# RWKV-7 recurrence on one core: grouping the chunk's state products, alternating the masked products, decay totals by head pairs

## The chip, the cores and the metric

The kernel runs on one core of one Trainium2 chip. The metric is device microseconds of one execution; the median of several executions counts. Engines are named as the profile names them: PE is TensorE (PEld its weight loads), DVE is VectorE, ACT is ScalarE, POOL is GpSimd, SP is SyncE. Each engine works through its own list of instructions in order and waits on semaphores for the others.

## What is computed

One two-layer trunk over 256 frames and 2048 features. Layer 0 mixes tokens with RWKV-7, layer 1 with forgetting attention, and each is followed by a SwiGLU. The change touches the recurrence of layer 0 alone: 32 heads of 64 features, each with a 64x64 state that is carried over the frames.

```python
def wkv7_scan(r, w, k, v, a, b):
    # S_t = S_{t-1} diag(w_t) + (S_{t-1} a_t) b_t^T + v_t k_t^T,   y_t = S_t r_t
    def step(S, inp):
        r_t, w_t, k_t, v_t, a_t, b_t = inp
        sa = jnp.einsum('bhij,bhj->bhi', S, a_t)
        S = (S * w_t[:, :, None, :] + sa[..., None] * b_t[:, :, None, :]
             + v_t[..., None] * k_t[:, :, None, :])
        return S, jnp.einsum('bhij,bhj->bhi', S, r_t)
...
    kk = kk / jnp.maximum(jnp.sqrt(jnp.sum(kk * kk, axis=-1, keepdims=True)), 1e-12)
    k = k * (1.0 + (a - 1.0) * k_a)
    y = wkv7_scan(rh, wh, kh, vh, -kk, kk * ah)
```

## The kernel before, in words

**The stream of large products.** All large weight matrices pass through one planned stream. A weight block of 128x512 is fetched by SP, split by ACT into a rounded high part (`wh`, line 148) and by DVE into the remainder (`wl`, line 149), and then used by six matmuls: for each of two halves of the frames high x high (line 174), high x low (175) and low x high (176). Seven split blocks may stand ready ahead of PE.

**Work between them.** Everything else runs as Python generators. `S.gemm` calls `tick()` after every three large matmuls, and a tick takes each live generator one `yield` further. So the order on every engine is fixed when the program is built: a background matmul sits in PE's list behind the large matmuls that were issued before its tick. Where a loop waits for a generator to get somewhere (`S.until`), it ticks without large matmuls, and background work stands back to back in PE's list. Background work shares four PSUM banks (tiles named `bg`), taken with `S.take` and handed back with `S.give`.

**The recurrence.** The 32 heads are four groups of eight, the 256 frames two halves of two chunks of 64. Eight *units* (group g, half t) pass in order through four generators, each unit with two chunks c: `prepare` builds the decayed keys and the masked products, `solve` and `merge` invert the triangular system of each chunk and head with small 32x32 products, `chain` carries the state over the chunks, and `post` normalises. All this lies beside the stream's products r, w2, a2, g2 and o. With `half = [0:64, 64:128]` of the partitions, chunk c keeps its values on `vs = half[c]` and its keys and its system on `us = half[1 - c]`.

- Line 521 sums the log decays within a chunk (`ps`). Line 523 sums them over a whole chunk for each head (`pc`): eight products with 64 columns of weights each, both chunks as two moving columns. Line 539 turns the totals into `wc` with two ACT instructions per unit.
- Lines 584 to 603 transpose the keys and place them head by head with ACT copies; the last of these, line 603, writes `fkb` in four copies (chunk 0 then chunk 1, even then odd heads).
- Line 611 forms, for chunk c and head h, the product of `fkb` and `far`, both 64 rows high on `us`, into 128 output partitions. Four heads fill one PSUM bank. Line 613 multiplies a bank with the causal mask on DVE and writes `M`. The order is chunk by chunk: bank, one `yield`, mask, next bank.
- Line 765 multiplies `M` with the values and the state in `sv` (128 rows, 64 columns) into the `us` half of a bank `pb`; line 767, for all chunks but the first of a group (12 of 16), multiplies `far` with the state alone (64 rows, 64 columns) into the `vs` half. The two alternate head by head. ACT copies the `us` half (770), line 773 applies the inverse, ACT copies again (775), and lines 778 and 780 form the new state and the output. Line 780 adds to what line 767 wrote.

An f32 product stands in the trace as two matmul records, so the eight products of line 765 for a chunk are 16 records.

Of the kernel before, what the change touches and what calls it, by code (L numbers as in the profile page):

```python
# [11 lines left out]
AF = mybir.ActivationFunctionType  # L12
# [5 lines left out]
P = 128  # L18
# [5 lines left out]
C = 64  # L24
# [9 lines left out]
C_ID, C_TRI, C_IND, C_M, C_E, C_B8, C_LANE, C_I8, C_CAUSAL, C_END = 0, 128, 256, 258, 386, 450, 482, 486, 550, 678  # L34
# [164 lines left out]
def hybrid_kernel(ctx, tc, const, x, a_norm_g, a_mix, a_w_rkv, a_w0, a_w1, a_w2, a_a0, a_a1, a_a2,  # L199
                  a_g1, a_g2, a_k_k, a_k_a, a_r_k, a_lnx_g, a_lnx_b, a_w_o, b_norm_g, b_w_in, b_b_f,  # L200
                  b_qn_g, b_kn_g, b_on_g, b_w_o, f_norm_g, f_w_gu, f_w_d, final_g, out):
    nc = tc.nc
# [33 lines left out]
    S = Stream(tc, ctx, plan, 4)  # L236
    mm = nc.tensor.matmul
# [15 lines left out]
    cst = small.tile([P, C_END], F32, name="cst")  # L253
# [72 lines left out]
    with ExitStack() as actx:  # L326
# [5 lines left out]
        with ExitStack() as bctx:  # L332
# [123 lines left out]
            b = begin()  # L456
# [25 lines left out]
        with ExitStack() as bctx:  # L482
# [22 lines left out]
            half = [slice(0, C), slice(C, P)]  # L505
            hsl = [slice(h * N, h * N + N) for h in range(8)]
# [5 lines left out]
            def prepare():  # L512
                for i, (g, t) in enumerate(order):
# [5 lines left out]
                    ps = yield from S.take()  # L519
                    pc = yield from S.take()  # L520
                    mm(ps[:, :], cst[:, C_TRI : C_TRI + P], tw[:, :], start=True, stop=True)
                    for h in range(8):
                        mm(pc[0:C, 2 * h : 2 * h + 2], tw[:, hsl[h]], cst[:, C_IND : C_IND + 2], start=True, stop=True)
                    kk = u1.tile([P, 512], F32, name="kk")
                    nc.vector.tensor_tensor(kk[:, :], k, vk[:, :], op=ALU.mult)
                    sq = u1.tile([P, 512], F32, name="rr")
# [9 lines left out]
                    nc.scalar.activation(W, ps[:, :], AF.Exp)  # L536
                    nc.scalar.activation(Wi[:, :], ps[:, :], AF.Exp, scale=-1.0)
                    for c in range(2):
                        nc.scalar.activation(wc[half[c], :], pc[0:C, c : 16 + c : 2], AF.Exp)
                    S.give(2)  # L540
                    n8 = u1.tile([P, 8], F32, name="n8")
                    nc.vector.tensor_reduce(n8[:, :], h4(sq[:, :]), AX.X, ALU.add)
# [60 lines left out]
                            nc.scalar.copy(dst, tkv[half[q], :, :])  # L603
                        S.give()
                    yield
                    for c in range(2):
                        us = half[1 - c]
                        for b in range(2):
                            pm = yield from S.take()
                            for h in range(4):  # L610
                                mm(pm[:, h * P : (h + 1) * P], fkb[us, b * 4 + h, :], far[us, b * 4 + h, :], start=True, stop=True)  # L611
                            yield
                            nc.vector.tensor_tensor(
                                M[:, c * 8 + b * 4 : c * 8 + b * 4 + 4, :], pm[:, :].rearrange("p (h n) -> p h n", n=P),
                                cst[:, C_M : C_M + P].unsqueeze(1).broadcast_to([P, 4, P]), op=ALU.mult,
                            )
                            S.give()
# [119 lines left out]
            def chain():  # L737
                nxt = values(0, 0, 0)
                for i, (g, t) in enumerate(order):
# [11 lines left out]
                    for c in range(2):  # L751
                        first = t == 0 and c == 0
                        last = t == 1 and c == 1
                        vs, us = half[c], half[1 - c]
                        sv, vu = nxt
                        vus.append(vu)
                        if c == 0:
                            nxt = values(g, t, 1)
                        elif i < 7:
                            if i:  # L760
                                yield from wait(("gated", i - 1))
                            nxt = values(*order[i + 1], 0)
                        pb = yield from S.take()
                        for h, hs in enumerate(hsl):
                            mm(pb[us, hs], M[:, c * 8 + h, C : 2 * C], sv[:, hs], start=True, stop=True)  # L765
                            if not first:
                                mm(pb[vs, hs], far[us, h, 0:C], sv[us, hs], start=h == 0, stop=False)  # L767
                        yield
                        yield
                        nc.scalar.copy(vu[us, :], pb[us, :])  # L770
                        pu = yield from S.take()
                        for h, hs in enumerate(hsl):
                            mm(pu[us, hs], TT[us, h, :], vu[us, hs], start=True, stop=True)  # L773
                        yield
                        nc.scalar.copy(vu[us, :], pu[us, :])
                        for h, hs in enumerate(hsl):
                            if not last:
                                mm(pu[vs, hs], kb[:, c, hs], vu[:, hs], start=True, stop=True)  # L778
                        for h, hs in enumerate(hsl):
                            mm(pb[vs, hs], M[:, c * 8 + h, 0:C], vu[:, hs], start=first, stop=first or h == 7)  # L780
                        if not last:
                            new = nxt[0][vs, :]
                            w = wc[vs, :].unsqueeze(2).broadcast_to([C, 8, N])
                            if first:
                                nc.vector.tensor_tensor(h4(new), h4(pu[vs, :]), w, op=ALU.mult)
                            else:
                                nc.vector.tensor_tensor(new, pu[vs, :], sv[us, :], op=ALU.add)
                                nc.vector.tensor_tensor(h4(new), h4(new), w, op=ALU.mult)
                        nc.scalar.copy(Y[vs, :], pb[vs, :])
                        S.give(2)  # L790
                        yield
                        yield
# [529 lines left out]
```

## Time and profile before

| | |
|---|---|
| median of 3 executions | 2687.72 us (2664.91 to 2695.59) |
| the profiled execution | 2667.2 us |
| its span, first to last instruction | 2665.4 us |
| mean granted PE clock over the span | 0.989 |
| PEld busy | 80% |
| DVE busy | 63% |
| ACT busy | 55% |
| POOL busy | 3% |
| DMA, mean | 176 GB/s |

The profiled execution is near the fastest of the three, and 20.5 us below their median. A busy PE is not PE at its peak: matmuls are pipelined and their ends are modelled, so the length of a run of matmuls is best read from the start of its first row to the start of the row that follows it. The recurrence fills about 256 to 640 us of the span; what comes before and after it holds no line of the change.

### The profile page before, as it was taken

How to read it: one execution, taken by the hardware profiler on the slowest of the kernel's cores; microseconds unless marked ns; L12 is line 12 of the kernel's file. 1: busy time of each engine (PE TensorE's matmuls, PEld its weight loads, DVE VectorE, ACT ScalarE, POOL GpSimd, SP SyncE). 2: the span in 40 equal slices, each digit the busy share in tenths (PEclk: the TensorE clock that was granted, in tenths of full speed). 3: DMA queues.
4: the chain of work that ended last, by engine and by line, in shares of the span. 5: the costliest groups of instructions: out<-in, count | busy, mean ns of one | idle time of the engine just before them, and what ended most of it. 6: DMA issues, size and time to landing. Idle time of an engine off the chain costs nothing.

```text
span 2665.4 us, 41151 instructions
## 1 busy us (share of the span) xinstructions
PE 2624.3 (98%) x15256; PEld 2142.5 (80%) x15256; DVE 1677.5 (63%) x2977; ACT 1478.7 (55%) x2849; POOL 87.9 (3%) x68
## 2 busy tenths in 40 slices
PE   7999999999999999999999999999999999999998
PEld 6788777777888888888888888888888888888886
DVE  7885876766655555555556677776755555555554
ACT  6665676756655545444445565665655555454443
POOL 0000010000000000000000110110000000000000
PEclk9999998889999999999999999999999999999999
DMA  5676332323666666665557666665566666665554
GB/s 187 193 215 206 99 100 79 92 91 111 178 194 185 193 187 191 187 193 191 192 191 205 202 193 184 196 185 170 174 192 186 192 187 191 187 191 193 196 195 157
DMA packets 253946, 468.48 MB, mean 176 GB/s; under 512 B 22248, under 2 KB 32696, under 8 KB 253744
## 3 DMA queue, kind: packets, MB, share of 16 engines
q1 hardware_dynamic: 251056, 464.58, 57.5%
q8 instruction: 120, 1.97, 0.3%
q10 hardware_dynamic: 2528, 1.26, 0.2%
q14 instruction: 82, 0.67, 0.1%
q0 software_dynamic: 160, 0.00, 0.0%
HBM read 457.37 MB, written 4.23 MB: 173 GB/s over the span
## 4 chain that ended last, share of the span: by engine, by line
PE 95%; ACT 2%; DVE 1%; DMA 1%; issue 1%; SPq 0%; ACTq 0%; POOLq 0%; DVEq 0%
PE mm L174 28%; PE mm L176 28%; PE mm L175 28%; PE bg L611 1%; PE bg L765 1%; PE bg L767 1%; DMA st<-in_a_w_rkv_dram 1%; PE bg L941 1%; ACT xb L592 1%; PE bg L773 1%; PE bg L302 1%; PE bg L778 1%; PE bg L780 0%; ACT Bs L811 0%; PE bg L1174 0%
## 5 line engine op out<-in xcount | busy, mean ns | idle before, releaser
L149 DVE TENSOR_TENSOR wl<-st,wh 128x512 fp32r<-128x512 f32 (+1 forms) x1648 | 1130.2, 691 | 823.1 <-ACT wh L148 817.8
L148 ACT CAST wh<-st 128x512 fp32r<-128x512 f32 (+1 forms) x1648 | 1018.8, 623 | 944.9 <-DVE wl L149 695.7
L174 PE MATMUL mm<-wh,xb 128*128 128x512 f32 x2048 | 803.6, 392 | 0.0
L176 PE MATMUL mm<-wh,xb 128*128 128x512 f32 x2048 | 799.8, 391 | 0.0
L175 PE MATMUL mm<-wl,xb 128*128 128x512 f32 x2048 | 799.4, 390 | 0.0
L174 PEld LDWEIGHTS mm<-wh,xb 128*128 128x128 f32 x2048 | 384.6, 188 | 79.9 <-issue 3.3
L176 PEld LDWEIGHTS mm<-wh,xb 128*128 128x128 f32 x2048 | 384.4, 188 | 79.5
L175 PEld LDWEIGHTS mm<-wl,xb 128*128 128x128 f32 x2048 | 384.7, 188 | 76.0
L174 PE MATMUL mm<-wh,xa 128*128 128x512 f32 x768 | 311.2, 406 | 0.0
L175 PE MATMUL mm<-wl,xa 128*128 128x512 f32 x768 | 307.4, 400 | 0.7 <-DVE wl L149 0.7
L176 PE MATMUL mm<-wh,xa 128*128 128x512 f32 x768 | 306.0, 399 | 0.0
L174 PE MATMUL mm<-wh,hb 128*128 128x512 f32 x448 | 174.3, 389 | 0.0
L175 PE MATMUL mm<-wl,hb 128*128 128x512 f32 x448 | 174.3, 389 | 0.0
L176 PE MATMUL mm<-wh,hb 128*128 128x512 f32 x448 | 174.3, 389 | 0.0
L174 PEld LDWEIGHTS mm<-wh,xa 128*128 128x128 f32 x768 | 146.4, 191 | 30.4 <-issue 1.0
L176 PEld LDWEIGHTS mm<-wh,xa 128*128 128x128 f32 x768 | 146.2, 191 | 30.4 <-DVE xa L854 0.2
L175 PEld LDWEIGHTS mm<-wl,xa 128*128 128x128 f32 x768 | 146.6, 191 | 29.2 <-DVE wl L149 1.5
L175 PEld LDWEIGHTS mm<-wl,hb 128*128 128x128 f32 x448 | 84.1, 188 | 17.5
L174 PEld LDWEIGHTS mm<-wh,hb 128*128 128x128 f32 x448 | 84.1, 188 | 17.4
L176 PEld LDWEIGHTS mm<-wh,hb 128*128 128x128 f32 x448 | 84.1, 188 | 17.4
L1122 POOL TENSOR_TENSOR n<-n,pw 128x8 f32<-128x8 f32 x24 | 45.1, 1882 | 411.4 <-DVE n L1121 411.4
L315 DVE TENSOR_TENSOR x<-mm,x 128x512 f32<-128x512 f32 x58 | 38.0, 685 | 11.6 <-PE mm L176 11.5
(277 smaller groups left out, 2007.7 us busy)
## 6 DMA issues: line engine op xcount, KB each, us to landing
st<-in_f_w_gu_dram SPq DMA_DIRECT2D x352, 512.0 KB
st<-in_f_w_d_dram SPq DMA_DIRECT2D x176, 512.0 KB
st<-in_b_w_in_dram SPq DMA_DIRECT2D x128, 512.0 KB
st<-in_a_w_rkv_dram SPq DMA_DIRECT2D x96, 512.0 KB
st<-in_a_w_o_dram SPq DMA_DIRECT2D x32, 512.0 KB
st<-in_b_w_o_dram SPq DMA_DIRECT2D x32, 512.0 KB
x<-in_x_dram SPq DMA_DIRECT2D x16, 256.0 KB
cb<-cdram SPq DMA_DIRECT2D x4, 1024.0 KB
```

What stands on the lines that cost most here:

```text
L148: nc.scalar.copy(hi[:rows, :n], st)
L149: nc.vector.tensor_tensor(lo[:rows, :n], st, hi[:rows, :n].bitcast(F32), op=ALU.subtract)
L174: nc.tensor.matmul(ps[t][:, :n], xh[:rows, c], wh, start=kt == 0, stop=False)
L175: nc.tensor.matmul(ps[t][:, :n], xh[:rows, c], wl, start=False, stop=False)
L176: nc.tensor.matmul(ps[t][:, :n], xl[:rows, c], wh, start=False, stop=kt == kts - 1)
L302: nc.tensor.transpose(tp[:, i * T + t * P : i * T + (t + 1) * P], src[:, t, c : c + P], ident)
L315: nc.vector.tensor_tensor(X[g][:, t, :], ps[t][:, :], X[g][:, t, :], op=ALU.add)
L592: nc.scalar.copy(dst, tpv[half[q], :, c, :])
L611: mm(pm[:, h * P : (h + 1) * P], fkb[us, b * 4 + h, :], far[us, b * 4 + h, :], start=True, stop=True)
L765: mm(pb[us, hs], M[:, c * 8 + h, C : 2 * C], sv[:, hs], start=True, stop=True)
L767: mm(pb[vs, hs], far[us, h, 0:C], sv[us, hs], start=h == 0, stop=False)
L1122: nc.gpsimd.tensor_tensor(n8[:, :], n8[:, :], pw[:, :], op=ALU.pow)
```

## The change

Three edits in two generators.

In `prepare`, the decay totals are formed for pairs of heads: four products with 128 columns of weights in place of eight with 64. The totals of odd heads then lie on the upper partitions, and `wc` is written with four ACT instructions in place of two.

Also in `prepare`, the masked products take two PSUM banks at once, one for each chunk, and alternate between the chunks head by head. Two masks follow together. The loop goes over two pairs of banks in place of four banks, with a `yield` each, so a unit has two yields there in place of four.

In `chain`, the eight products of line 765 are issued first and the eight of line 767 after them, in place of alternating.

```diff
-                    for h in range(8):
-                        mm(pc[0:C, 2 * h : 2 * h + 2], tw[:, hsl[h]], cst[:, C_IND : C_IND + 2], start=True, stop=True)
+                    for p in range(4):
+                        mm(pc[:, 2 * p : 2 * p + 2], tw[:, p * P : (p + 1) * P], cst[:, C_IND : C_IND + 2], start=True, stop=True)
...
                     for c in range(2):
-                        nc.scalar.activation(wc[half[c], :], pc[0:C, c : 16 + c : 2], AF.Exp)
+                        for q in range(2):
+                            nc.scalar.activation(wc[half[c], q:8:2], pc[half[q], c:8:2], AF.Exp)
...
-                    for c in range(2):
-                        us = half[1 - c]
-                        for b in range(2):
-                            pm = yield from S.take()
-                            for h in range(4):
-                                mm(pm[:, h * P : (h + 1) * P], fkb[us, b * 4 + h, :], far[us, b * 4 + h, :], start=True, stop=True)
-                            yield
+
+                    for b in range(2):
+                        pm = []
+                        for c in range(2):
+                            pm.append((yield from S.take()))
+                        for h in range(4):
+                            for c in range(2):
+                                us = half[1 - c]
+                                mm(pm[c][:, h * P : (h + 1) * P], fkb[us, b * 4 + h, :], far[us, b * 4 + h, :], start=True, stop=True)
+                        yield
+                        for c in range(2):
                             nc.vector.tensor_tensor(
-                                M[:, c * 8 + b * 4 : c * 8 + b * 4 + 4, :], pm[:, :].rearrange("p (h n) -> p h n", n=P),
+                                M[:, c * 8 + b * 4 : c * 8 + b * 4 + 4, :], pm[c][:, :].rearrange("p (h n) -> p h n", n=P),
                                 cst[:, C_M : C_M + P].unsqueeze(1).broadcast_to([P, 4, P]), op=ALU.mult,
                             )
                             S.give()
...
                         for h, hs in enumerate(hsl):
                             mm(pb[us, hs], M[:, c * 8 + h, C : 2 * C], sv[:, hs], start=True, stop=True)
-                            if not first:
+                        if not first:
+                            for h, hs in enumerate(hsl):
                                 mm(pb[vs, hs], far[us, h, 0:C], sv[us, hs], start=h == 0, stop=False)
```

## The prediction, on record before the changed kernel ran

> **What bounds the kernel now.** I read the page's totals and its chain of waits first, then the busy table over the stretch of the recurrence, then PE's timeline inside it.
>
> ```profile
> span 2665.4 us, 41151 instructions
> ...
> PE 95%; ACT 2%; DVE 1%; DMA 1%; issue 1%; SPq 0%; ACTq 0%; POOLq 0%; DVEq 0%
> ```
>
> PE holds 95% of the chain that ended last. Now the busy table for 256 to 660 us: length, busy time of PE, PEld, DVE, ACT and POOL (instructions in brackets), PE's granted clock, DMA share, GB/s.
>
> ```profile
> 256.00:660.00 404.00, 394.84 (x4943) 304.01 (x4942) 292.52 (x622) 274.73 (x678) 32.98 (x25) 0.94 0.31 95
> ```
>
> PE is busy for 394.84 of 404 us, DVE for 292.52 (72%) and ACT for 274.73 (68%). DMA stands at 0.31 of its time, so the weights are no limit here. What shortens PE's list in this stretch shortens the kernel, as long as DVE and ACT keep up. The second thing to see is the clock, 0.94 in place of 1.
>
> PE's timeline shows what line 765 and 767 cost (start, length, engine, line, count of records):
>
> ```profile
> 316.95 1.15 PE L765 MATMUL bg<-sv,xb 128*64 128x64 f32 x16
> 318.03 0.50 PE L175 MATMUL mm<-wl,xa 128*128 128x512 f32 x1
> ...
> 325.16 0.33 PE L765 MATMUL bg<-sv,xb 128*64 128x64 f32 x2
> 325.42 0.32 PE L767 MATMUL bg<-sv,xb 64*64 64x64 f32 x2
> 325.68 0.33 PE L765 MATMUL bg<-sv,xb 128*64 128x64 f32 x2
> ...
> 329.27 0.50 PE L175 MATMUL mm<-wl,xa 128*128 128x512 f32 x1
> ...
> 330.41 1.14 PE L773 MATMUL bg<-vu,TT 64*64 64x64 f32 x16
> 331.48 0.50 PE L176 MATMUL mm<-wh,xa 128*128 128x512 f32 x1
> ```
>
> Alone, the 16 records of line 765 take 318.03 - 316.95 = 1.08 us. Alternating with line 767, each product of two records takes 0.26 us, and the 32 records take 329.27 - 325.16 = 4.11 us. The 16 records of line 773, which have line 767's shape and stay in one shape, take 331.48 - 330.41 = 1.07 us. So the change of shape at every product costs about half of the 4.11 us.
>
> **The change part by part.**
>
> *State products in one run (765, 767).* Per chunk: 1.08 + 1.07 = 2.15 us by the two rows above, in place of 4.11. That is 1.96 us for each of 12 chunks, 23.5 us. Upper end the same: the shapes stay what they are. Lower end 0, if the slowness belonged to line 767 itself; line 773's row speaks against that. ACT, which takes the result, waits for PE here and not PE for ACT: in its group of the stretch (busy time and mean ns, then idle time before it and what ended it) the copy of line 770 waits 36.4 us in all for line 767.
>
> ```profile
> L770 ACT COPY vu<-bg 64x512 f32<-64x512 f32 x16 | 9.3, 582 | 36.6 <-PE bg L767 36.4
> ```
>
> *Granted clock.* The busy table for six of the twelve alternating runs (start and end by the timeline), with the sum of all:
>
> ```profile
> 325.16:329.27 4.11, 4.11 (x33) 3.03 (x33) 2.23 (x7) 0.03 (x1) 0.00 (x0) 1.00 0.01 5
> ...
> 409.59:414.24 4.65, 4.65 (x33) 3.37 (x33) 3.74 (x10) 0.28 (x1) 0.00 (x0) 0.84 0.49 156
> 443.33:447.73 4.40, 4.40 (x34) 3.22 (x33) 3.54 (x8) 4.10 (x11) 1.94 (x1) 0.90 0.19 63
> 497.35:501.46 4.11, 4.11 (x34) 3.03 (x33) 3.59 (x14) 1.31 (x4) 0.00 (x0) 1.00 0.51 150
> ...
> 536.85:543.31 6.46, 6.46 (x34) 4.58 (x33) 1.93 (x4) 0.56 (x3) 0.00 (x0) 0.50 0.00 0
> ...
> 592.60:596.71 4.11, 4.11 (x34) 3.03 (x33) 2.49 (x12) 0.62 (x2) 0.00 (x0) 1.00 0.31 79
> ...
> sum 52.47, PE 52.47 PEld 38.45 DVE 34.64 ACT 17.12 POOL 3.89; mean PE 4.37 PEld 3.20 DVE 2.89 ACT 1.43 POOL 0.32
> ```
>
> The same table for the five stretches of the recurrence in which the granted clock was 0.50:
>
> ```profile
> 412.75:422.99 10.24, 10.24 (x59) 7.96 (x60) 2.60 (x6) 1.78 (x3) 0.24 (x1) 0.50 0.10 34
> 446.88:450.30 3.42, 3.42 (x12) 2.67 (x11) 2.84 (x7) 1.85 (x4) 0.00 (x0) 0.50 0.21 50
> 501.50:508.32 6.82, 6.82 (x34) 5.02 (x34) 0.00 (x0) 2.82 (x5) 0.00 (x0) 0.50 0.28 101
> 525.39:545.87 20.48, 20.48 (x115) 15.17 (x113) 11.44 (x22) 11.42 (x29) 1.95 (x1) 0.50 0.12 35
> 597.07:603.90 6.83, 6.83 (x39) 5.12 (x38) 1.67 (x4) 2.52 (x5) 0.00 (x0) 0.50 0.27 100
> ```
>
> Four of the five drops begin within an alternating run or at most 0.4 us after its end (412.75, 446.88, 501.50, 597.07). The four last 27.3 us, and at half clock half of it is lost: 13.7 us. The fifth (20.48 us) begins in other work at 525.39, but the run at 536.85 lies within it; I count 4 us of its 10.2 as won. All lengths are multiples of 3.41 us, so a drop seems to be decided window by window, and an alternating run of 4.11 us can fill a window where one of 2.15 us can't. I take 17.7 us; ends 0 (the drops come from something that stays) and 23.9 (half of all 47.8 us). The drops need not repeat alike in another execution: the one profiled took 2667.2 us, 20.5 us less than the median of 2687.72.
>
> [...]
>
> *Masked products (611).* One unit, PE with the ACT copies that it waits for:
>
> ```profile
> 308.76 2.38 ACT L603 COPY WW<-bg 64x512 f32<-64x512 f32 x4
> 309.39 0.48 PE L611 MATMUL bg<-xb,WW 64*128 64x128 f32 x2 [0.16 <-ACT WW L603]
> 309.80 0.50 PE L174 MATMUL mm<-wh,xa 128*128 128x512 f32 x1
> 310.23 0.93 PE L611 MATMUL bg<-xb,WW 64*128 64x128 f32 x6
> 311.10 0.69 PE L704 MATMUL bg<-Ti,xb 32*32 32x32 f32 x32
> 311.72 2.60 PE L611 MATMUL bg<-xb,WW 64*128 64x128 f32 x24
> 314.25 1.12 PE L521 MATMUL bg<-tw,cst 128*128 128x512 f32 x2
> 315.31 1.09 PE L523 MATMUL bg<-cst,tw 128*64 128x2 f32 x16
> 316.33 0.69 PE L720 MATMUL bg<-Tt,Xs 32*32 32x32 f32 x32
> ```
>
> And line 611's own records in two equal stretches of its long run:
>
> ```profile
> 312.16:312.72 0.56, 0.56 (x11) 0.56 (x10) 1.00 0.00 0
> 313.10:313.66 0.56, 0.56 (x7) 0.56 (x7) 1.00 0.00 0
> ```
>
> Line 611 takes 0.41 + 0.87 + 2.53 = 3.81 us per unit. The two stretches hold 11 records where the run passes from chunk 0 to chunk 1, hence from one half of the rows to the other, against 7 inside a chunk (records that reach into a stretch are counted). So products on different row halves run side by side, and a change of half costs nothing. Alternating them at every head would double the rate: 16 records as 8 steps of about 0.11 us (2.53/24) and 0.2 us to start (0.87 - 6 x 0.11), 1.1 us for a bank pair, 2.2 per unit, 12.9 us over 8 units. That is the upper end. The lower end takes the alternation as dear as that of 765 and 767, 0.26 us for each of 16 products: 4.2 us per unit, 3 us lost in all.
>
> I take less than the upper end, since the first bank pair now needs all four copies of line 603, where the first bank needed two. They end at 308.76 + 2.38 = 311.14. PE waits there in order, with line 704 and the large products behind it, and ACT's line 708 waits for 704; five of the eight products can follow only then (0.6 us), so line 704 starts at about 311.8, the second pair at 312.4, and the end is 313.5 in place of 314.25. That is 0.7 us per unit, 5.6 us in all.
>
> *Masks (613) and banks.* The same 32 DVE instructions, in pairs:
>
> ```profile
> L613 DVE TENSOR_TENSOR xb<-bg,cst 128x512 f32<-128x512 f32 x32 | 21.6, 687 | 9.3 <-PE bg L611 9.3
> ```
>
> A pair takes 1.4 us, so the second bank of a pair comes free 0.7 us later than it would alone, and two banks are held where one was. `merge` holds a third. PE's next use of a bank may wait a part of that: up to 8 x 0.7 = 5.6 us, none if line 704 or a large product lies between. I take 2 us.
>
> *Decay totals (523, 539).* Line 523 takes 316.33 - 315.31 = 1.02 us for 16 records. It becomes 8 records with twice the weight columns, at the shape of the neighbours, so the change of shape goes too. Ends: half, 0.51 us less per unit (4 us in all), and nothing, if a record costs by its weight columns. I take 1 us. For line 539 the row gives the shortest, median and longest of its 16 instructions in ns:
>
> ```profile
> L539 ACT ACTIVATE wc<-bg x16: 163/170/172, 258.5 to 537.3; 64x8 f32<-64x8 f32 x16
> ```
>
> Sixteen more at 0.17 us are 2.7 us of ACT, with the weight casts of line 148 queued behind them; I count 1 us as exposed, ends 0 and 2.7.
>
> *Less cover.* The stretch loses about 48 us of PE, while DVE and ACT keep their work: 292.52 of 356 us is 82%. Seven split blocks stand ready ahead of PE, so most of it stays hidden. In the alternating runs DVE works 34.64 of 52.47 us; they shrink to 12 x 2.15 = 25.8 us and would hold 17.0 of it in the same proportion. The other 17.6 us must find room elsewhere: ends 0 and 17.6; I take 2 us, since DVE has 111 us free in the stretch.
>
> Sum against the profiled execution: 2667.2 - 23.5 - 17.7 - 5.6 - 1 + 2 + 1 + 2 = 2624.4, rounded to 2624 us. That is 1.6% below it and 2.4% below the median shown.
>
> **The rivals.**
>
> *Masked products at full worth.* If the ACT copies are not what PE waits for, 12.9 in place of 5.6: 2617 us. For it: PE's wait on line 603 in this unit is 0.16 us. Against: its first bank needs two copies only.
>
> *The drops of the clock stay.* Small products remain, and the fifth drop began without an alternating run ahead. Then the 17.7 us are missing: 2642 us. Against: four of five begin with one. [...]
>
> *DVE or ACT becomes the bound.* If the 17.6 us of "less cover" are lost in place of 2: 2640 us. For it: DVE's 72% rises to 82%, and ACT's share likewise. Against: ACT waits for PE in its row, 36.4 us before line 770 alone, and gets those waits back.
>
> *The order changes nothing.* If the 0.26 us per product came from line 767's operands and not from the alternation, 23.5 and 17.7 us are missing: 2666 us. Against: line 773's row.
>
> [...]
>
> **How the numbers follow.** Chances: the forecast 0.56, masked products at full worth 0.09, drops stay 0.15, DVE or ACT 0.12, nothing changes 0.05, slower 0.03. The predicted time is the forecast's, 2624 us. The range, 2604 to 2652, takes in the first four. It reaches up to 10 us over the higher of the two at 2640 and 2642 and down to where all drops go (6 us more) and the masked products bring their full worth (7 us more), with 7 us for what two executions differ by. About 1% is what a measurement of this kernel can tell from no change. The forecast and the first rival are faster by more (0.65), and so are the two at 2640 and 2642 us against the median shown (1.7%), but not against an execution like the profiled one (0.9%); I give two thirds of their 0.27 to faster. So faster 0.83, within 1% 0.14 (with "nothing changes"), slower 0.03.
>
> **What would show it.** Right: line 765 and line 767 as two runs of 16 records, together 2.1 to 2.2 us; no half clock behind them, and a granted clock over 0.97 for the recurrence; line 611 as runs of 16 in 1.1 us, with the first of a unit held up by line 603; line 523 as 8 records in 0.9 us. Wrong: 767 still at 0.26 us a product; half clock behind single runs; PE waiting often for `wl` or `wh`, which would mean that DVE and ACT set the pace; a unit's line 611 over 3.8 us.

## The result, and the profile after

The changed kernel takes 2629.93 us in the median (four executions, 2625.47 to 2637.86) against 2678.70 us for the kernel before (four executions, 2664.91 to 2695.59): a ratio of 0.983, with an interval of 0.980 to 0.987. The profiled execution took 2628.21 us, 39 us less than the profiled one of before. One execution of e2 below, of 5686 us where the nine others took 2674 to 2691, is left out of every figure here. Six lines that matter have new numbers: 603 is now 604, 611 is 615, 613 is 618, 765 is 770, 767 is 773 and 773 is 779.

The page of the changed kernel, its first line and the shares of its chain of waits:

```profile
span 2626.4 us, 41027 instructions
...
PE 92%; ACT 4%; DVE 2%; issue 1%; DMA 1%; POOL 0%; SPq 0%; ACTq 0%; POOLq 0%; DVEq 0%
```

The busy table (length; busy time of PE, PEld, DVE, ACT, POOL; granted clock; DMA share; GB/s) for the recurrence and for what follows it:

```profile
256.00:623.00 367.00, 351.86 (x4897) 278.09 (x4896) 294.88 (x630) 278.13 (x699) 35.90 (x25) 0.99 0.35 107
623.00:2626.00 2003.00, 1990.22 (x9165) 1640.25 (x9163) 1187.20 (x1945) 1042.57 (x1848) 51.28 (x33) 1.00 0.62 189
```

The ends at 660 us (before) and 623 us (changed) do not fall on the same work: the large product of the stream that starts at 660 us before starts at 619.3 us here. By the same products the recurrence is 40.7 us shorter, and what follows it 1 to 2 us longer. DVE and ACT do in 367 us about what they did in 404, so DVE is busy for 80% of the stretch and ACT for 76%. PE still carries the chain, but ACT's share of it rose from 2% to 4% and DVE's from 1% to 2%. PE is idle for 367.00 - 351.86 = 15.1 us there, where it was 9.2 us.

PE's timeline for the state products:

```profile
324.05 1.15 PE L770 MATMUL bg<-sv,xb 128*64 128x64 f32 x16
325.13 1.14 PE L773 MATMUL bg<-sv,xb 64*64 64x64 f32 x16
326.20 0.50 PE L175 MATMUL mm<-wl,xa 128*128 128x512 f32 x1
```

326.20 - 324.05 = 2.15 us. The timeline of one unit's masked products and decay totals, with the ACT copies ahead of them:

```profile
340.01 2.39 ACT L604 COPY WW<-bg 64x512 f32<-64x512 f32 x4
340.64 0.49 PE L615 MATMUL bg<-xb,WW 64*128 64x128 f32 x2
341.06 0.50 PE L174 MATMUL mm<-wh,xa 128*128 128x512 f32 x1
341.49 1.90 PE L615 MATMUL bg<-xb,WW 64*128 64x128 f32 x14
343.32 0.69 PE L709 MATMUL bg<-Ti,xb 32*32 32x32 f32 x32
343.94 1.16 PE L615 MATMUL bg<-xb,WW 64*128 64x128 f32 x16
345.03 1.12 PE L521 MATMUL bg<-tw,cst 128*128 128x512 f32 x2
...
346.45 0.95 PE L523 MATMUL bg<-cst,tw 128*128 128x2 f32 x8
347.26 0.49 PE L174 MATMUL mm<-wh,xa 128*128 128x512 f32 x1
```

The first pair of banks takes 0.42 + 1.83 = 2.25 us and ends 0.9 us after the fourth copy (342.40), the second pair 1.09 us. Line 523 takes 0.81 us.

The busy table for all the stretches of the recurrence with the clock at half:

```profile
310.15:313.56 3.41, 3.41 (x30) 2.60 (x24) 2.03 (x4) 2.60 (x7) 0.00 (x0) 0.50 0.00 0
388.65:392.07 3.42, 3.42 (x9) 2.63 (x9) 3.28 (x8) 3.33 (x8) 0.00 (x0) 0.50 0.02 5
572.97:576.39 3.42, 3.24 (x15) 2.14 (x16) 1.45 (x3) 2.76 (x7) 1.46 (x1) 0.50 0.54 155
sum 10.25, PE 10.07 PEld 7.38 DVE 6.75 ACT 8.69 POOL 1.46; mean PE 3.36 PEld 2.46 DVE 2.25 ACT 2.90 POOL 0.49
```

47.8 us of half clock became 10.25 us. The starts of the stretches lie a whole number of windows apart (388.65 - 310.15 = 78.5 = 23 x 3.413; 572.97 - 388.65 = 184.3 = 54 x 3.413), and so do those of before (446.88 - 412.75 = 34.13 = 10 x 3.413). In each of these two executions all drops of the recurrence start on one grid of 3.413 us. The grid does not start with the kernel: counted in whole windows from the first instruction, the drops lie 2.95 us past one here (310.15), 3.15 us in the kernel before (412.75), and below 2.63 us in e2 (361.03) and 0.23 us in e12 (310.84).

The second of these drops stands behind a wait that the kernel before did not have. Timeline, with the wait in brackets:

```profile
386.19 1.28 DVE L618 TENSOR_TENSOR xb<-bg,cst 128x512 f32<-128x512 f32 x2
...
386.93 1.05 PE L523 MATMUL bg<-cst,tw 128*128 128x2 f32 x8 [1.37 <-DVE xb L618]
```

Line 523 needs the bank that the first of two masks hands back. The first drop follows a window with 2.35 us of masked products, the third a pause of PE of 1.39 us before line 709, for which the profile names no releaser. In the view of waits for this stretch the row of line 523 is new (engine and line, what it waited for, us in total, times, longest):

```profile
PE bg L615 <- ACT WW L604: 2.2, 6, 0.8
...
PE bg L523 <- DVE xb L618: 1.4, 1, 1.4
```

Between the two profiled executions, from start to start in PE's timeline, the state products went from 56.7 to 30.0 us, the masked products from 33.9 to 28.2, line 523 from 9.0 to 7.3.

### The profile page after: what moved, and what is told of

It is laid out like the page before. It is cut to its first block, busy times and chain, and to the rows that moved or that the text cites. A ratio compares the mean times of both kernels' runs of the same rounds, so it can differ in the third digit from the quotient of the medians.

```text
span 2626.4 us, 41027 instructions
## 1 busy us (share of the span) xinstructions
PE 2578.1 (98%) x15192; PEld 2113.7 (80%) x15192; DVE 1674.5 (64%) x2977; ACT 1475.4 (56%) x2865; POOL 91.4 (3%) x68
## 4 chain that ended last, share of the span: by engine, by line
PE 92%; ACT 4%; DVE 2%; issue 1%; DMA 1%; POOL 0%; SPq 0%; ACTq 0%; POOLq 0%; DVEq 0%
PE mm L174 28%; PE mm L176 28%; PE mm L175 28%; PE bg L947 1%; PE bg L779 1%; ACT xb L593 1%; PE bg L770 1%; PE bg L615 1%; PE bg L786 1%; PE bg L302 1%; ACT wh L148 1%; DVE wl L149 1%; PE bg L784 0%; PE bg L773 0%; ACT Bs L817 0%
## 5 line engine op out<-in xcount | busy, mean ns | idle before, releaser
L174 PE MATMUL mm<-wh,xb 128*128 128x512 f32 x2048 | 803.6, 392 | 0.0
L175 PE MATMUL mm<-wl,xb 128*128 128x512 f32 x2048 | 799.5, 390 | 0.0
L174 PEld LDWEIGHTS mm<-wh,xb 128*128 128x128 f32 x2048 | 384.7, 188 | 79.8 <-issue 3.3
L175 PEld LDWEIGHTS mm<-wl,xb 128*128 128x128 f32 x2048 | 384.8, 188 | 75.9
L174 PE MATMUL mm<-wh,xa 128*128 128x512 f32 x768 | 306.6, 400 | 0.0
L175 PE MATMUL mm<-wl,xa 128*128 128x512 f32 x768 | 304.6, 397 | 0.8 <-DVE wl L149 0.8
L174 PE MATMUL mm<-wh,hb 128*128 128x512 f32 x448 | 174.3, 389 | 0.0
L175 PE MATMUL mm<-wl,hb 128*128 128x512 f32 x448 | 174.3, 389 | 0.0
L175 PEld LDWEIGHTS mm<-wl,xa 128*128 128x128 f32 x768 | 145.1, 189 | 29.4 <-DVE wl L149 1.5
L174 PEld LDWEIGHTS mm<-wh,xa 128*128 128x128 f32 x768 | 145.2, 189 | 29.3 <-issue 1.0
L174 PEld LDWEIGHTS mm<-wh,hb 128*128 128x128 f32 x448 | 84.1, 188 | 17.4
L175 PEld LDWEIGHTS mm<-wl,hb 128*128 128x128 f32 x448 | 84.1, 188 | 17.4
L360 DVE SCALAR_TENSOR_TENSOR xmf<-xx,gcol,hT 128x256 f32<-128x256 f32 x96 | 43.7, 479 | 0.2
```

The lines of the kernel that those rows point to most:

```text
L174: nc.tensor.matmul(ps[t][:, :n], xh[:rows, c], wh, start=kt == 0, stop=False)
L175: nc.tensor.matmul(ps[t][:, :n], xh[:rows, c], wl, start=False, stop=False)
L360: nc.vector.scalar_tensor_tensor(f[:, :], xx[:, kt, :], gcol[:, c : c + 1], hT[:, kt, 1 : T + 1], op0=ALU.mult, op1=ALU.add)
```

## The experiments

**A measure that takes the clock out.** Every execution has its granted clock beside its time. Half clock in one execution is 2 x (1 - clock) x span; the granted clock in the traces of before and of the changed kernel is either 1.00 or 0.50. Over 45 executions of the kernel before, which ran beside the experiments, time = 2644.5 us + 0.426 x half clock (correlation 0.98); one at clock 0.993 took 2659.52 us, one at 0.979 took 2693.65 us. So the clock makes nearly all the spread of this kernel. The table gives each kernel's mean half clock, and its time with 0.426 of it taken off. One execution keeps about 1.7 us of scatter after that (the standard deviation of the 45), the mean of four about 0.8. In the traces 9 to 13 us of half clock lie at the start and the end of an execution. The kernel before ran in three groups, one beside each group of experiments, and comes out at 2644.4, 2644.5 and 2644.8 us without the clock, so rows of different groups can be compared; the changed kernel was measured by itself.

| kernel | median us | ratio to before (95%) | half clock us | without it us |
|---|---|---|---|---|
| before (45 executions) | 2675.2 | 1 | 75.7 | 2644.5 |
| changed | 2629.9 | 0.983 (0.980 to 0.987) | 32 | 2617.3 |
| e1_state | 2636.2 | 0.984 (0.979 to 0.988) | 36 | 2619.3 |
| e2_masks | 2678.2 | 1.001 (0.999 to 1.004) | 92 | 2641.1 |
| e3_totals | 2669.0 | 0.998 (0.995 to 1.000) | 65 | 2642.9 |
| e4_split | 2674.6 | 0.999 (0.995 to 1.003) | 70 | 2644.7 |
| e5_twos | 2643.5 | 0.987 (0.982 to 0.991) | 38 | 2626.4 |
| e6_noalt | 2630.2 | 0.981 (0.976 to 0.986) | 33 | 2617.7 |
| e7_dvecopy | 2630.2 | 0.982 (0.978 to 0.986) | 26 | 2619.0 |
| e9_shape | 2622.8 | 0.981 (0.976 to 0.986) | 34 | 2608.1 |
| e10_merge | 2616.5 | 0.977 (0.973 to 0.981) | 24 | 2606.9 |
| e11_mergeonly | 2633.2 | 0.984 (0.979 to 0.990) | 45 | 2612.5 |
| e12_gap | 2670.4 | 0.998 (0.994 to 1.002) | 54 | 2648.4 |

A difference between two medians holds some microseconds of clock. The last column compares the work alone.

### e1: the chain's edit alone

```diff
                             mm(pb[us, hs], M[:, c * 8 + h, C : 2 * C], sv[:, hs], start=True, stop=True)
-                            if not first:
+                        if not first:
+                            for h, hs in enumerate(hsl):
                                 mm(pb[vs, hs], far[us, h, 0:C], sv[us, hs], start=h == 0, stop=False)
```

> Only the edit in the chain: the products of line 765 in one run, then those of line 767. Theory (the change of shape at every product is the cost, and the drops of the granted clock follow from it): the two lines take 2.15 us per chunk in place of 4.11, no stretch at half clock begins behind them, and the time falls by 33 to 45 us, nearly all of what the whole change brings. Rival (the masked products bring a good part): it falls by less than 28 us. Rival (drops come from something else): lines 765 and 767 at 2.15 us, but still over 35 us at half clock, and the time falls by 20 to 26 us.

Measured: 38.5 us less in the median than the kernel before beside it (2674.70). Without the clock it is 25.2 us (2644.5 - 2619.3). The half clock falls from 75.7 to 36 us. This edit alone brings all but 6 us of the whole in the median, and all but 2 us of it without the clock.

### e2: the masked products alone

```diff
-                    for c in range(2):
-                        us = half[1 - c]
-                        for b in range(2):
-                            pm = yield from S.take()
-                            for h in range(4):
...
+                    for b in range(2):
+                        pm = []
+                        for c in range(2):
+                            pm.append((yield from S.take()))
+                        for h in range(4):
+                            for c in range(2):
+                                us = half[1 - c]
```

> Only the masked products: two banks at once, the chunks alternating head by head. Theory (the first pair of banks waits for the copies into fkb): the line's records shrink by 5 to 7 us in all, the second pair of a unit takes 1.1 us, the first 2.2 us, lines 765 and 767 stay at 4.11 us with drops of the clock behind some of them; the time falls by 0 to 8 us, hard to tell from none. Rival (full worth): the first pair takes 1.1 us too and the time falls by 11 to 15 us. Rival (alternating rows costs like alternating shapes): a pair takes 2.1 us or more and the time rises.

Measured: no difference in the median that is clear of the scatter, and 3.4 us less without the clock, since this kernel ran with 92 us of half clock. Its trace is the best place to see what brings a drop. Nine drops fall in its recurrence; seven have a window of 3.41 us just before them in which state products stand for 3.0 us or more. The busy table of those seven windows, for the instructions that read `sv` alone, first and last of them and the sum:

```profile
357.62:361.03 3.41, 3.11 (x25) 2.31 (x25) 0.00 (x0) 0.00 (x0) 1.00 0.23 67
...
640.92:644.33 3.41, 3.41 (x28) 2.46 (x26) 0.00 (x0) 0.00 (x0) 1.00 0.49 138
sum 23.87, PE 22.35 PEld 16.32 DVE 0.00 POOL 0.00; mean PE 3.19 PEld 2.33 DVE 0.00 POOL 0.00
```

At a clock of 1.00, PE counts as busy with alternating products for 22.35 of 23.87 us, and after each of these windows the granted clock was 0.50.

### e3: the decay totals alone

```diff
-                    for h in range(8):
-                        mm(pc[0:C, 2 * h : 2 * h + 2], tw[:, hsl[h]], cst[:, C_IND : C_IND + 2], start=True, stop=True)
+                    for p in range(4):
+                        mm(pc[:, 2 * p : 2 * p + 2], tw[:, p * P : (p + 1) * P], cst[:, C_IND : C_IND + 2], start=True, stop=True)
```

> Only the decay totals by pairs of heads. Theory: line 523 takes 0.88 us per unit in place of 1.02, 1 us in all, against 2.7 us more of ACT: the time moves by less than 3 us either way. Rival (the two changes of shape around line 523 count, 0.15 us each for 8 units): it falls by 3 to 4 us.

Measured: 1.6 us less without the clock, about three standard errors; 4.5 of the median's 6 us are clock (65 against 75.7 us). Line 523 fell from 9.0 to 7.0 us in PE's list. The rest of the edit is as in the change.

### e4: the alternation broken in the middle

```diff
                                 mm(pb[vs, hs], far[us, h, 0:C], sv[us, hs], start=h == 0, stop=False)
+                            if h == 3 and not first:
+                                yield
```

> The kernel before with one more yield after the fourth head in the alternation of lines 765 and 767, so that large matmuls stand between two alternating runs of 2.05 us. Theory (a drop of the clock comes when an alternating run fills a window of 3.41 us): lines 765 and 767 still cost 0.26 us a product, but no half clock begins behind them; less than 15 us at half clock in the recurrence in place of 47.8, and the time falls by 8 to 20 us. Rival (the drops come from something else): 30 to 60 us at half clock remain and the time moves by less than 4 us.

This run tells nothing. Of the 12 chunks only one was split in PE's list, which the timeline shows; the other eleven stand as before, four products and four more in one run. The order of PE's list is therefore not simply that of the ticks, as the part on the kernel before had it: background products even stand between lines 174 and 175 of one block, where no tick is (the state products of the changed kernel above, which end at an L175, begin behind an L174 at 323.73). So instructions are put in another order somewhere between the kernel's text and PE; no run here shows where. A `yield` alone doesn't separate them. e12 forces it.

### e5: alternating by twos

```diff
-                        for h, hs in enumerate(hsl):
-                            mm(pb[us, hs], M[:, c * 8 + h, C : 2 * C], sv[:, hs], start=True, stop=True)
...
+                        for h0 in range(0, 8, 2):
+                            for h in (h0, h0 + 1):
+                                mm(pb[us, hsl[h]], M[:, c * 8 + h, C : 2 * C], sv[:, hsl[h]], start=True, stop=True)
```

and the same by twos for the products of line 767 (773 in the changed kernel), all on top of the changed kernel.

> The changed kernel, with lines 765 and 767 alternating by twos (two heads of the one, two of the other), so that the shape changes 8 times per chunk in place of 2. Theory (each change of shape costs about 0.15 us): a chunk takes 3.0 us in place of 2.15, 10 us more over 12 chunks, so 2636 to 2644 us. A run of 3.0 us can seldom fill a window of 3.41 us: under 20 us at half clock. Rival (the cost lay in alternating single heads, for instance in the order of their operands): 2.2 to 2.4 us per chunk and 2628 to 2634 us.

The timeline of one chunk:

```profile
324.85 0.45 PE L771 MATMUL bg<-sv,xb 128*64 128x64 f32 x4
325.22 0.44 PE L774 MATMUL bg<-sv,xb 64*64 64x64 f32 x4
325.60 0.45 PE L771 MATMUL bg<-sv,xb 128*64 128x64 f32 x4
...
327.84 0.50 PE L175 MATMUL mm<-wl,xa 128*128 128x512 f32 x1
```

Four records take 0.374 us where the pace inside a run, 0.0585 us from one record's start to the next (line 776 in e10, 327.33 to 328.09 us for 13 records), would give 0.23. In the kernel before a piece of two takes 0.26 in place of 0.12, and a run of 16 takes 1.08 in place of 0.94 (16 x 0.0585). In all three the surplus is 0.14 us: the same for each change of shape at pieces of 2, 4 and 16 records. It lost 9.1 us without the clock against the changed kernel, near the 10 expected. Its half clock, 38 us in the mean, is above what was expected: with about 11 at the ends taken off, 27 us stay.

### e6 and e7: what the masked products wait for

e6 keeps two banks and two masks together, but puts chunk 0's four heads before chunk 1's:

```diff
-                        for h in range(4):
-                            for c in range(2):
-                                us = half[1 - c]
+                        for c in range(2):
+                            us = half[1 - c]
+                            for h in range(4):
```

> The changed kernel, masked products still in two banks at a time, but first the four heads of chunk 0, then the four of chunk 1. Theory (products on the two row halves run side by side when they alternate; the first pair of banks is bound by the copies into fkb): the second pair takes 1.8 to 2.0 us in place of 1.09, the first pair stays within 0.3 us of 2.25; the time rises by 3 to 8 us over the changed kernel. Rival (nothing runs side by side): the pairs take the same time as before and the time stays.

```profile
347.79 0.48 PE L615 MATMUL bg<-xb,WW 64*128 64x128 f32 x2 [0.20 <-ACT WW L604]
...
348.64 1.90 PE L615 MATMUL bg<-xb,WW 64*128 64x128 f32 x14
350.47 0.69 PE L709 MATMUL bg<-Ti,xb 32*32 32x32 f32 x32
351.10 1.71 PE L615 MATMUL bg<-xb,WW 64*128 64x128 f32 x16
352.73 1.13 PE L521 MATMUL bg<-tw,cst 128*128 128x512 f32 x2
```

In this timeline the first pair is as long as in the changed kernel (0.42 + 1.83), the second 1.63 us in place of 1.09. So the alternation by heads shortens the second pair, by 0.54 us a unit or 4.3 us over eight (0.7 to 0.9 a unit were expected), and yet the kernel is not slower (2617.7 against 2617.3 us without the clock, each to within about 1 us), where 3 to 8 us were expected. The busy table up to the large product at which the changed kernel's 623 us fall:

```profile
256.00:637.60 381.60, 371.00 (x4901) 295.35 (x4901) 296.71 (x632) 280.97 (x702) 34.84 (x25) 0.94 0.34 103
```

PE is idle for 381.60 - 371.00 = 10.6 us, in the changed kernel for 15.1. So in these two traces what the alternation takes out of PE's list comes back as waiting.

e7 moves half of the copies that hold the first pair from ACT to DVE:

```diff
-                            nc.scalar.copy(dst, tkv[half[q], :, :])
+                            if q == 0:
+                                nc.scalar.copy(dst, tkv[half[q], :, :])
+                            else:
+                                nc.vector.tensor_copy(dst, tkv[half[q], :, :])
```

> The changed kernel, with the two odd-head copies into fkb of each unit on DVE in place of ACT. Theory (the first pair of banks waits for the fourth copy on ACT): the first pair of banks takes 1.2 to 1.8 us in place of 2.25, and the time falls by 2 to 8 us below the changed kernel. Rival (DVE is as full as ACT here, and the masks behind the copies come later): the time stays or rises by up to 5 us.

The timeline of one unit's first pair:

```profile
417.28 0.48 PE L618 MATMUL bg<-xb,WW 64*128 64x128 f32 x2 [0.28 <-ACT WW L605]
...
417.69 0.50 PE L176 MATMUL mm<-wh,xa 128*128 128x512 f32 x1
...
418.13 0.48 PE L618 MATMUL bg<-xb,WW 64*128 64x128 f32 x2
...
418.54 0.50 PE L174 MATMUL mm<-wh,xa 128*128 128x512 f32 x1
...
419.20 1.26 PE L618 MATMUL bg<-xb,WW 64*128 64x128 f32 x12
420.39 0.69 PE L712 MATMUL bg<-Ti,xb 32*32 32x32 f32 x32
```

With the copies shared out, large products stand between the pieces, and 12 records take 1.19 us where 14 took 1.83. In sum this first pair takes 0.41 + 0.41 + 1.19 = 2.01 us in place of 2.25; over the units 1.4 to 2.0, apart from one in which the clock was half, where 1.2 to 1.8 were expected. So the copies held the first pair, in part at least. The time is the same (2619.0 us without the clock), as the rival expected. Whether the shorter wait is worth nothing or DVE's added work took it back is not settled: the waits of PE in e7 begin with a row that the changed kernel lacks.

```profile
PE mm L176 <- DVE xa L863: 3.6, 1, 3.6
```

### e9 and e10: the shape alone, and the products in another place

e9 is the kernel before with line 767 at line 765's shape. It reads all 128 rows, and the other 64 add a foreign term to the product:

```diff
-                                mm(pb[vs, hs], far[us, h, 0:C], sv[us, hs], start=h == 0, stop=False)
+                                mm(pb[vs, hs], far[:, h, 0:C], sv[:, hs], start=h == 0, stop=False)
```

> The kernel before, with line 767 alternating with line 765 as before, but over all 128 rows, so that both have the shape 128 rows by 64 columns and differ in the column half only. The other rows bring a foreign term into the product, so the output isn't the reference's; the number of instructions is the same. Theory (the change of shape is the cost, not the alternation): the 32 records of a chunk take 1.1 to 1.3 us in place of 4.11, side by side, and the time falls by 40 to 60 us, more than with the two runs. Rival (alternating the output half costs as much): still 4 us and no change.

```profile
325.09 0.27 PE L765 MATMUL bg<-sv,xb 128*64 128x64 f32 x1
325.09 0.27 PE L767 MATMUL bg<-sv,xb 128*64 128x64 f32 x1
...
326.17 0.50 PE L175 MATMUL mm<-wl,xa 128*128 128x512 f32 x1
```

The timeline has both lines alternating record by record, starting together. 32 records take 326.17 - 325.09 = 1.08 us, where they took 4.11: same order, same count, more rows, but one shape and the two column halves of the array. So the cost was the change of shape and not the alternation.

e10 uses this in the changed kernel: line 767's products go down to line 773's (of before), which have the same 64x64 shape and write the other column half.

```diff
-                        if not first:
-                            for h, hs in enumerate(hsl):
-                                mm(pb[vs, hs], far[us, h, 0:C], sv[us, hs], start=h == 0, stop=False)
                         yield
...
                             mm(pu[us, hs], TT[us, h, :], vu[us, hs], start=True, stop=True)
+                            if not first:
+                                mm(pb[vs, hs], far[us, h, 0:C], sv[us, hs], start=h == 0, stop=False)
```

> The changed kernel, with the products of line 767 moved down and alternating with those of line 773, which have the same shape (64 rows, 64 columns), the same row half and the other column half. Theory (a change costs only when the shape changes, and products on different column halves run side by side): the 32 records of a chunk take 1.1 to 1.4 us in place of 2.15 in two places, about 10 us over 12 chunks: 2616 to 2624 us. Rival (a common row half keeps them one after the other): 1.9 to 2.1 us for the 32, one change of shape less, and 2625 to 2632 us. Rival (the other column half counts as a change): 4 us for the 32 and 2645 us or more.

```profile
327.17 0.27 PE L776 MATMUL bg<-vu,TT 64*64 64x64 f32 x1
327.18 0.27 PE L778 MATMUL bg<-sv,xb 64*64 64x64 f32 x1
...
328.25 0.50 PE L176 MATMUL mm<-wh,xa 128*128 128x512 f32 x1
```

Both together take 328.25 - 327.17 = 1.08 us, so line 767 adds nothing to PE's list any more (line 773's 16 records alone took 1.07). Without the clock this is 10.4 us below the changed kernel. Its median, 2616.47 us, is the lowest of all kernels here, the changed one included.

The runs together: 0.14 us went with a change of shape (before and e5), nothing with a change of half at one shape (e9), and two column halves ran side by side in 1.08 us (e9 and e10).

### e11: that edit without the other two

The kernel before with e10's edit of the chain alone; the diff is the same, from the alternating lines.

> The kernel before with line 765 alone and line 767 alternating with line 773, without the edits of the masked products and the decay totals. Theory (these two bring 2 to 5 us together, apart from drops of the clock): 2 to 6 us over the kernel with all three, 2618 to 2626 us, 50 to 58 us below the kernel before. Rival (the masked products in pairs cost as much as they bring): within 2 us of 2616.

Measured: 5.6 us over e10 without the clock, near the parts e2 and e3 (3.4 + 1.6). The median, 2633.2, lies outside what was expected, because its executions had 45 us of half clock against 24.

### e12: the alternation broken for certain

A DVE instruction between the halves adds nothing to `sv` (zero times the first results) but must run before the second half:

```diff
+                            if h == 3 and not first:
+                                nc.vector.scalar_tensor_tensor(
+                                    sv[us, 256:512], pb[us, 0:256], 0.0, sv[us, 256:512], op0=ALU.mult, op1=ALU.add
+                                )
+                                yield
```

> The kernel before, with the alternation of lines 765 and 767 broken after the fourth head by a dependency: DVE adds zero times the first half's result to the state of the heads to come, so the second half can start only after that, and five large matmuls stand between. Theory (a drop of the clock comes when an alternating run fills a window of 3.41 us, and a run of 2.05 us can't): 0.26 us a product as before, but 15 to 45 us at half clock per execution in place of about 76, none of the drops behind these lines, and 2655 to 2668 us in place of 2675. Rival (the drops have another cause): 60 us or more at half clock remain and the time is 2675 us or more, since DVE has 12 instructions more.

Timeline of one chunk, then the half clock of its recurrence in the busy table:

```profile
336.27 0.33 PE L767 MATMUL bg<-sv,xb 64*64 64x64 f32 x2
336.52 0.50 PE L175 MATMUL mm<-wl,xa 128*128 128x512 f32 x1
...
337.57 0.40 PE L176 MATMUL mm<-wh,xa 128*128 128x512 f32 x1
337.90 0.33 PE L765 MATMUL bg<-sv,xb 128*64 128x64 f32 x2
```

```profile
310.84:327.90 17.06, 17.06 (x135) 13.40 (x135) 8.39 (x18) 10.22 (x24) 0.00 (x0) 0.50 0.02 8
...
sum 54.61, PE 54.61 PEld 43.01 DVE 31.86 ACT 38.66 POOL 0.71; mean PE 10.92 PEld 8.60 DVE 6.37 ACT 7.73 POOL 0.14
```

Every chunk is split now, and of its five drops none follows a window full of state products (one has 1.01 us of them in it). But the half clock is 54 us in the mean, where 15 to 45 was expected, and the median, 2670.4 us, lies just above its range. The rival's 60 us and 2675 us weren't met either. 3.9 us of it are the DVE instruction and the splits (2648.4 against 2644.5), and drops that began elsewhere stand where those others did. So a kernel without such windows can still lose much to the clock. The drop at 310.84 follows a window in which PE was idle for 1.28 us, and lasts five windows.

**All drops counted.** Four traced kernels alternate for 4.11 us at a stretch (before, e2, e3, e4). They have 27 drops in the recurrence, and 22 of these follow a window with 2.84 us or more of alternating state products. The nine others have 23 drops, none of that kind. Of the 23, 12 follow a window with 1.8 us or more of masked products, 9 more one with over 1 us of PE idle, and 2 neither. An estimate from these numbers: a run of 4.11 us covers at least 2.84 us of one window of the grid in (4.11 - 2.84 + 3.41 - 2.84) / 3.41 = 54% of its positions, or 6.5 of 12 runs, 26 of 48. The four traces have 25 such windows, and 2.15 us can never reach it.

Counted the other way, from the windows of the grid at full clock between 256 and 680 us, this is a graded effect. In the four kernels a drop follows all 19 windows with more than 3.1 us of state products that alternate one by one, 3 of the 6 with 2.84 to 3.1 us, and none of the 23 with 2.0 to 2.84. The other two kinds of window say much less: over the thirteen traces a drop follows 14 of 104 windows with 1.8 us or more of masked products, 12 of 27 with over 1 us of PE idle, and 3 of 1321 with none of the three. e5 has five windows with 2.85 to 3.06 us of products that alternate by twos, none with a drop behind it; against 3 of 6 that is too few to tell.

## Why the prediction was right

The forecast was 2624 us, the median is 2629.9, inside the range and on the predicted side. Without the term for the clock the forecast's terms sum to 25.1 us, and 27.2 us were measured without the clock (2644.5 - 2617.3). No term is off by more than 1.7 us (the state products, 25.2 for 23.5). But the small terms are hardly larger than the scatter of the runs, and one of them, the masked products, may have come out for another reason than the one given. Step by step:

- **State products in one run, 23.5 us.** Right. 2.15 us per chunk, as predicted, and 25.2 us from e1 without the clock. The reason given, the change of shape, is shown by e9: alternation at one shape costs 1.08 us for both. The rival "the order changes nothing" is out.
- **Granted clock, 17.7 us.** Right in size: mean half clock fell from 75.7 to 32 us, and 0.426 of it is 18.6 us. Between the two profiled executions, which the forecast started from, it fell by 47.8 - 10.25 = 37.5 us in the recurrence, 16 us of time. The prediction took half of the half clock as lost; the slope says 0.426. Right too in where drops begin: behind windows that alternating products fill, 22 of 27 drops and all 19 windows with more than 3.1 us. How much half clock goes with them is less sure, since e12 has no such window and keeps 54 us; that the size came out so near is in part luck. The rival "the drops stay" is out for this kernel. But three drops stayed in the profiled execution, and the prediction named no cause for them; 32 us less the 12 at the ends leaves 20 us, 8.5 us of time. With none, the kernel would take about 2617.3 + 0.426 x 12 = 2622 us.
- **Idle time before a drop.** PE is busy in the records for 22.35 of 23.87 us before seven drops of e2, so those seven came without PE idle in the sense of the records, in which the ends of matmuls are modelled. Nor was any window before a drop in the recurrence idle throughout: the most idle one has 2.94 of 3.41 us, in e7.
- **Masked products 5.6 us, masks and banks 2 us lost.** The sum, 3.6 us gained, was met: 3.4 us in e2. So was PE's own list (33.9 to 28.2 us), though not in each unit: 3.81 us became 2.25 + 1.09 = 3.34 in the one shown, 0.47 us in place of 0.7. The reason holds for the first pair, which ends soon after the fourth copy. What was missed is that PE's gain there is worth little: e6 gives back half a microsecond in each unit and loses no time, PE only waits less. So the 3.4 us need not come from the alternation, and that they equal the sum is in part luck. The edit also halves the unit's yields, two in place of four, which may let the generator get on sooner; no run tries this alone. "Masked products at full worth" is out. The bank wait was seen once, 1.37 us at line 523, with a drop behind it.
- **Decay totals, 0 (1 us won, 1 us lost).** 1.6 us gained in e3. Line 523's 0.81 us is a little under the 0.9 predicted, and PE's list lost 2.0 us by it in e3 in place of 1; ACT's two more instructions in each unit cost nothing that can be seen.
- **Less cover, 2 us.** Not shown by itself. The three parts alone sum to 30.2 us (25.2 + 3.4 + 1.6), together they bring 27.2; the 3 us between are about twice their own error (an estimate, 1.3 us, from the scatter of the runs), and no run ties them to cover. The rival "DVE or ACT becomes the bound" is out for the changed kernel, since e10 still gains 10.4 us from PE's list. PE's idle time, 15.1 us in place of 9.2, did not come with the lost cover alone: e1, which loses most of it, has 8.2 us idle in its recurrence, and e6 10.6.
- **Slower, 0.03.** Out: the ratio is 0.983, and no drop followed the longer runs in one shape that the change makes.

What stays open: what brings a drop. The windows before drops hold many changes of shape and slow products at once; e9 takes both away together, so no run here tells them apart. Why e12's half clock stays at 54 us, and what the masked products have to do with the drops that follow some of them, is open too. Nor was it tried to remove the drops behind PE's waits.

## What to carry to other kernels

Put small products of one array shape next to one another, and place products of the same shape on the other column or row half of the array beside them: 0.14 us went with each change of shape in the kernel before and e5, two column halves took the time of one, 1.08 us, in e9 and e10, and row halves alternating took 1.09 us where e6, one half after the other, took 1.63. Before comparing kernels that differ by 1%, read the granted clock of every execution; here it explained most of a spread from 2660 to 2694 us, and a slow stretch of small products cost once in its length (4.11 us in place of 2.15) and a second time in the clock behind it (a drop followed all 19 windows with more than 3.1 us of it). A shorter list on PE need not make a shorter kernel, even where PE holds 92% of the chain: in e6 its gain turned into waiting.

## What the runs showed of the hardware that was not expected

A whole group of products came for nothing: line 767's 16 records add 0.01 us to line 773's in e10, where they cost 1.07 us alone. A change of shape had one price, 0.14 us, for pieces of 2 and 16 records (before) and of 4 (e5). Half-clock time was not half lost: the slope over 45 executions is 0.426, not 0.5. That some of it lies beside waits for other engines would fit, but wasn't tested. And short pauses of PE had drops behind them: one followed 12 of 27 windows with 1.0 to 2.94 us of idle time.
